# Row tiles of the token norm in the x^T buffers, double buffers for T and its copy, U and X copies of 132 columns, six PSUM places for w_in

## The chip, the cores and the metric

The kernel runs on one core of one Trainium2 chip. The metric is the device time in microseconds (us) of one execution. A time is the median of several runs of the same program. Below, PE stands for TensorE, DVE for VectorE, ACT for ScalarE, POOL for GpSimd and SP for SyncE, whose queue issues most of the DMA transfers of the first half.

## The reference

One layer of a streaming encoder is computed for 1024 prompt tokens and 32 sample tokens, 1056 columns in all. Both pass through the same layer: a norm over each token, one input projection w_in (1024 inputs), and two branches that read its output, a state-space branch (S5, 32 groups of 16 channels, 64 complex states each) and a latent attention branch (MLA). The sample tokens start from given states and a given cache.

```python
def mixer_layer(x, pos, h0, past_ckv, past_krope, p):
    h = rmsnorm(x, p['norm_in'])
    z = h @ p['w_in']
    u, g_ssm, c_q, c_kv, k_rope_raw, g_mla = jnp.split(z, cuts, axis=-1)
    y_ssm, h_last = s5_branch(u, h0, p)
    q = (rmsnorm(c_q, p['q_lora_norm']) @ p['w_uq']).reshape(...)
    ...
    mix = jnp.concatenate([rmsnorm(y_ssm, p['out_norm_ssm']) * jax.nn.silu(g_ssm),
                           rmsnorm(attn, p['out_norm_mla']) * jax.nn.silu(g_mla)], axis=-1)
    return x + mix @ p['w_out'], ckv, krope, h_last

def s5_branch(u, h0, p):
    ...
    bu = jnp.einsum('gpc,bsgc->bsgp', b_bar, ug.astype(jnp.complex64))
    _, states = lax.associative_scan(_ssm_combine, (a_seq, bu), axis=1)
    y = jnp.einsum('gcp,bsgp->bsgc', c_mat, states).real
    y = y + p['ssm_d'] * ug
    yg = jax.nn.gelu(y)
    out = yg * jax.nn.sigmoid(yg @ p['w_glu'] + p['b_glu'])
```

## The kernel before

**The input projection.** x arrives transposed, in eight tiles of 128 features by 1056 columns (`xr`). Each is split into a high and a low part (`xh` by ACT, `xl` by DVE), as are the weights (`wh`, `wl`). A tile m of w_in is 128 output rows: three PSUM chunks of 384, 384 and 288 columns, each the sum over eight k of three products (`wh*xh`, `wh*xl`, `wl*xh`), 72 matmuls named `mt` at L235 in all. The tiles m = 0 to 3 give u, eight more give the two gates. The PSUM chunks come from the tag "g" with `CAP["g"]` places. The projection runs on x without the token norm; the factor 1/rms of each token is applied when a chunk leaves PSUM (`mtile_evac`, on DVE, against the tile `rb`).

**The token norm.** x is read a second time in rows (nine tiles `xk`, 128 tokens by 1024; L279 and L282), and ACT squares and sums each at L283. DVE turns the nine sums into 1/rms (the steps from L284 to L160), and PE spreads them over the partitions (`rb_p`, L185), from where ACT copies them to `rb` (L187). Tiles m = 0 and 1 end before `rb` is there; ACT copies them raw to `ur` (L298), and DVE scales them later into `uT` (L251).

**The state-space branch.** `uT` goes to DRAM (`du`) and comes back as `U`, 16 channels by 8 steps on the partitions, 132 columns for each of the 8 groups of a tile. A block of 8 steps is one column (4 of the sample, 128 of the prompt). `ssm_in(m)` builds the weights W and transposes them to `Gt` (`gt_p`, L469), forms the kernel parts `kpt` and `kp`, and multiplies `Gt` with U to `v_p` (L491); ACT copies v_p to X (L494, L495). A scan over the blocks runs on DVE in X. Then, for each m, the output `y_p` is the sum of two matmuls for each of 8 groups, `Tg * U` (L681) and `Hm * Xc` (L682). `Tg` is a reordered copy of T by ACT (L667), `Xc` a reordered copy of the states in X by ACT (L670). T, Tg and Xc have one buffer each. ACT applies gelu into `ysb` (L683), `ysb` goes to DRAM, returns as `yg`, is split into `ygh` and `ygl`, and feeds the gated unit's matmuls `gl` (L711).

**What sets the order.** The source's order is not the order of the engines. A scheduler puts the instructions of each engine into one fixed order, by data dependencies, by how many buffers and PSUM places each tag has, and by its own model of times; each engine then runs its list in order. So a change of a buffer count moves work on every engine. Marks (`issue_after`) keep some work behind a given instruction.

Of the kernel before, what the change touches and what calls it, by code (L numbers as in the profile page):

```python
# [50 lines left out]
def step(ctx: ExitStack, tc, xT, xr, winF, winT, wuq, wukv, wglu, wout, ckvcT, krcT, pk, rot, ssb, ssc, mtab,  # L51
# [5 lines left out]
    sb = ctx.enter_context(tc.tile_pool(name="sb", bufs=1))  # L57
    sm = ctx.enter_context(tc.tile_pool(name="sm", bufs=2))
    psS = ctx.enter_context(tc.tile_pool(name="psS", bufs=2, space=PSUM))
    CAP = {"a": 6, "b": 4, "g": 4, "w": 4}  # L60
    psA = ctx.enter_context(tc.tile_pool(name="psA", bufs=4, space=PSUM))
    dr = ctx.enter_context(tc.tile_pool(name="dr", bufs=1, space=DRAM))

# [210 lines left out]

    ssx = CC(TS)
    for i in range(TS):
        t = T("xk", [128, D], 3)
        if i < 8:
            sp.dma_start(t, xr[i * 128:i * 128 + 128])  # L279
        else:  # L280
            for j in range(4):
                sp.dma_start(t[32 * j:32 * j + 32], xr[NP_:])  # L282
        act.activation(t, t, AF.Square, accum_out=ssx[:, i:i + 1])  # L283
# [163 lines left out]
    XR = X.rearrange("p g (j s) -> p g j s", j=8)  # L447

    def load_u(m, after=None):

        t = T("U", [128, 4 + 8 * NCH], 2)
        dve.memset(t[:, 0:4], 0.0)
        with tc.issue_after(marks[after]) if after else nullcontext():
            sp.dma_start(t[:, 4:].rearrange("p (g n) -> p g n", n=NCH), du[m].rearrange("r c g n -> (r c) g n"))
        return t

    def ucol(t, g):

        return t[:, g * NCH:g * NCH + 136]

    def ssm_in(m):
        w = T("W", [128, 8, 128], 2)
# [24 lines left out]
        for g0 in (0, 3, 6):  # L487
            n = min(3, 8 - g0)
            p = PA("v_p")
            for j in range(n):  # L490
                pe.matmul(p[:, j * 136:(j + 1) * 136], gt[:, g0 + j, :], ucol(u, g0 + j), start=True, stop=True)  # L491
            pb = p[:, :n * 136].rearrange("p (g s j) -> p g j s", g=n, j=8)
            xg = XR[:, 8 * m + g0:8 * m + g0 + n]
            act.activation(xg[:, :, 1:8, 0:17], pb[:, :, 0:7], AF.Copy)  # L494
            act.activation(xg[:, :, 0, 1:18], pb[:, :, 7], AF.Copy)  # L495


    aq = T("aq", [128, 3, 4, G])
# [158 lines left out]


    for m in range(4):
        Tm = T("T", [128, L, 8, GC], 1)  # L660
        for s in range(L):
            o = (L - 1 - s) * 16
            with tc.issue_after(marks["so"]):
                sp.dma_start(Tm[:, s].rearrange("p g c -> p (g c)"), dk[o:o + 128, m * 128:(m + 1) * 128])

        Tg = T("Tg", [128, 8, L, GC], 1)
        act.activation(Tg.rearrange("p g s c -> p s g c"), Tm, AF.Copy)  # L667
        hm = T("Hm", [128, 8, 128], 2)
        xc = T("Xc", [128, 8, 136], 1)
        act.activation(xc.rearrange("p g (s j) -> p g s j", j=8),  # L670
                       XR[:, 8 * m:8 * m + 8, :, 0:17].rearrange("p g j s -> p g s j"), AF.Copy)
        with tc.issue_after(marks["scan"]):
            expand(hm.rearrange("p g (s c) -> p g s c", c=GC), ct[:, 0], ct[:, 1], m, pr, pi, dve)
        u = load_u(m, "so")
        ysb = T("ysb", [128, 8, NCH], 2)
        for g0 in (0, 3, 6):
            n = min(3, 8 - g0)
            p = PA("y_p")
            for j in range(n):
                o = p[:, j * 136:(j + 1) * 136]  # L680
                pe.matmul(o, Tg[:, g0 + j].rearrange("p s c -> p (s c)"), ucol(u, g0 + j), start=True, stop=False)  # L681
                pe.matmul(o, hm[:, g0 + j, :], xc[:, g0 + j], start=False, stop=True)  # L682
            act.activation(ysb[:, g0:g0 + n], p[:, :n * 136].rearrange("p (g c) -> p g c", c=136)[:, :, 4:],  # L683
                           AF.Gelu_apprx_tanh)
        sp.dma_start(dy[m].rearrange("s c g n -> (s c) g n"), ysb)


# [650 lines left out]
```

## Time and profile before

| | |
|---|---|
| median of 3 runs | 588.09 us (587.78 to 588.16) |
| the profiled execution's own time | 588.01 us |
| its span, first to last instruction | 586.2 us |
| PE busy | 548.5 us, 94% of the span |
| DVE busy | 416.4 us, 71% |
| ACT busy | 306.7 us, 52% |
| mean granted clock of PE | 0.974 |

The span leaves 1.8 us of the profiled time outside. The granted clock has two levels, 1.0 (2.4 GHz) and 0.5 (1.2 GHz); a value between them is a stretch that holds some of each. A line's busy time is the sum of its instructions; matmuls overlap, so that the busy time of PE is the time in which any of them runs.

### The profile page before, as it was taken

How to read it: one execution, taken by the hardware profiler on the slowest of the kernel's cores; microseconds unless marked ns; L12 is line 12 of the kernel's file. 1: busy time of each engine (PE TensorE's matmuls, PEld its weight loads, DVE VectorE, ACT ScalarE, POOL GpSimd, SP SyncE). 2: the span in 40 equal slices, each digit the busy share in tenths (PEclk: the TensorE clock that was granted, in tenths of full speed). 3: DMA queues.
4: the chain of work that ended last, by engine and by line, in shares of the span. 5: the costliest groups of instructions: out<-in, count | busy, mean ns of one | idle time of the engine just before them, and what ended most of it. 6: DMA issues, size and time to landing. Idle time of an engine off the chain costs nothing.

```text
span 586.2 us, 9933 instructions
## 1 busy us (share of the span) xinstructions
PE 548.5 (94%) x3707; PEld 481.0 (82%) x3707; DVE 416.4 (71%) x1008; ACT 306.7 (52%) x647; POOL 107.1 (18%) x165
## 2 busy tenths in 40 slices
PE   5995899999999999689999799999999999999897
PEld 4995799889999998689888678887778888876785
DVE  6998533989999355038999996669798677674722
ACT  5743145127242635649855975786675776653000
POOL 0000000000000010000024520032245244458430
PEclk9998899999999999679999899999999999999999
DMA  8992642222551007352301031200100101096362
GB/s 286 397 303 45 184 148 73 79 74 88 158 176 45 0 24 215 119 181 90 122 29 72 26 107 73 92 1 2 39 20 2 38 1 40 1 341 209 105 253 107
DMA packets 35265, 63.92 MB, mean 109 GB/s; under 512 B 5361, under 2 KB 21521, under 8 KB 35217
## 3 DMA queue, kind: packets, MB, share of 16 engines
q1 hardware_dynamic: 31008, 49.06, 25.6%
q10 hardware_dynamic: 4208, 14.22, 7.0%
q8 instruction: 29, 0.48, 0.3%
q14 instruction: 20, 0.16, 0.1%
HBM read 47.06 MB, written 16.21 MB: 108 GB/s over the span
## 4 chain that ended last, share of the span: by engine, by line
PE 76%; DVE 12%; ACT 4%; DMA 3%; issue 2%; POOL 2%; SPq 1%; ACTq 0%; POOLq 0%; DVEq 0%
PE mt L235 21%; PE wo L879 9%; PE ob L1054 6%; PE pt_p L1026 5%; PE S L986 3%; PE S L987 3%; PE S L988 3%; PE gl L711 3%; PE tk_p L590 2%; PE tk_p L591 2%; PE tk_p L592 2%; PE y_p L682 1%; PE ob L1055 1%; PE v_p L491 1%; DMA wr<-winF 1%
## 5 line engine op out<-in xcount | busy, mean ns | idle before, releaser
L235 PE MATMUL mt<-xh,wh 128*128 128x384 f32 (+1 forms) x288 | 78.3, 334 | 9.0 <-ACT xh L112 6.6
L235 PE MATMUL mt<-xl,wh 128*128 128x384 f32 (+1 forms) x288 | 77.6, 330 | 0.4 <-DVE xl L113 0.4
L235 PE MATMUL mt<-xh,wl 128*128 128x384 f32 (+1 forms) x288 | 76.7, 329 | 0.0
L235 PEld LDWEIGHTS mt<-xh,wh 128*128 128x128 f32 x288 | 51.3, 191 | 11.2 <-ACT xh L112 7.2
L235 PEld LDWEIGHTS mt<-xl,wh 128*128 128x128 f32 x288 | 51.3, 192 | 1.1 <-DVE xl L113 0.7
L235 PEld LDWEIGHTS mt<-xh,wl 128*128 128x128 f32 x288 | 50.8, 192 | 0.2 <-issue 0.2
L1026 PE MATMUL pt_p<-base,P 128*128 128x128 f32 x288 | 43.1, 276 | 0.7 <-ACT kv L775 0.7
L879 PE MATMUL wo<-woh,mm 128*128 128x512 f32 x128 | 42.0, 399 | 1.2 <-DVE mm L110 1.2
L1054 PE MATMUL ob<-PT,kv 128*64 128x128 f32 x576 | 41.9, 279 | 0.9 <-DVE PT L1030 0.9
L1054 PEld LDWEIGHTS ob<-PT,kv 128*64 128x64 f32 x576 | 32.0, 136 | 10.3 <-issue 6.5
L1008 DVE TENSOR_REDUCE base<-S 128x1 f32<-128x1024 f32 (+3 forms) x32 | 32.4, 1016 | 10.5 <-PE S L988 10.4
L742 POOL TENSOR_TENSOR base<-base 128x288 f32<-128x288 f32 x1 | 0.9, 862 | 211.3 <-DVE kro L638 211.3
L1010 ACT ACTIVATE P<-S,base 128x1024 f32<-128x1024 f32 (+3 forms) x32 | 30.5, 953 | 14.9 <-DVE base L1008 14.7
L1026 PEld LDWEIGHTS pt_p<-base,P 128*128 128x128 f32 x288 | 33.0, 140 | 5.1 <-ACT kv L775 0.9
L986 PE MATMUL S<-kTh,qTh 104*128 104x512 f32 (+3 forms) x96 | 36.1, 376 | 0.0
L1030 DVE COPY PT<-pt_p 128x512 f32<-128x512 f32 (+2 forms) x44 | 27.9, 634 | 9.5 <-PE pt_p L1026 8.5
L988 PE MATMUL S<-kTh,qTh 96*128 96x512 f32 (+3 forms) x96 | 34.2, 360 | 0.0
L987 PE MATMUL S<-kTl,qTh 96*128 96x512 f32 (+3 forms) x96 | 33.4, 348 | 0.0
L109 ACT ACTIVATE wh<-wr 128x512 fp32r<-128x512 f32 x24 | 14.0, 623 | 34.2 <-PE mt L235 29.6
L879 PEld LDWEIGHTS wo<-woh,mm 128*128 128x128 f32 x128 | 24.1, 190 | 7.1 <-DVE mm L110 1.6
L109 ACT ACTIVATE wt<-wtr 128x416 fp32r<-128x416 f32 x16 | 8.6, 554 | 36.8 <-PE tk_p L592 16.1
L825 POOL TENSOR_TENSOR qx<-q,base 128x256 f32<-128x256 f32 (+1 forms) x12 | 8.6, 731 | 104.0 <-DVE base L160 88.6
(344 smaller groups left out, 1449.2 us busy)
## 6 DMA issues: line engine op xcount, KB each, us to landing
wr<-winF SPq DMA_DIRECT2D x10, 512.0 KB, 4.5
U<-du SPq DMA_DIRECT2D x8, 528.0 KB, 4.0
xk<-xr SPq DMA_DIRECT2D x8, 512.0 KB, 7.7
wor<-wout ACTq DMA_DIRECT2D x8, 512.0 KB, 4.4
dyp<-yp SPq DMA_DIRECT2D x8, 512.0 KB, 2.6
part<-dyp ACTq DMA_DIRECT2D x8, 512.0 KB, 5.5
xt<-xr ACTq DMA_DIRECT2D x8, 512.0 KB, 7.3
xr<-xT SPq DMA_DIRECT2D x7, 528.0 KB, 7.9
```

The lines of the kernel that those rows point to most:

```text
L109: act.activation(hi, src, AF.Copy)
L235: pe.matmul(ps[c][:, :b - a], ww[:, k, :], xx[k][:, a:b], start=(k == 0 and first), stop=(k == 7 and last))
L711: pe.matmul(ps[c][:, :352], ww[:, k], xx[k][:, c * 352:(c + 1) * 352], start=(k == 0 and first), stop=(k == 3 and last))
L879: pe.matmul(s[i][c], mm[i][a][k], ww[k][b][:, c * 512:(c + 1) * 512], start=(k == 0 and first), stop=(k == 3 and last))
L986: pe.matmul(s[:, :n], qh[:, qj], kh[:, j, :n], start=True, stop=False)
L987: pe.matmul(s[:, :n], qh[:96, qj], kl[:, j, :n], start=False, stop=False)
L988: pe.matmul(s[:, :n], ql[:, qj], kh[:96, j, :n], start=False, stop=True)
L1008: dve.tensor_reduce(rl[:, 2 + j:3 + j], sf, AX.X, ALU.max, negate=True)
L1010: marks["exp", u] = act.activation(t[:, :n], sf, AF.Exp, bias=rl[:, 2 + j:3 + j], accum_out=rl[:, j:j + 1]).ins
L1026: pe.transpose(pp[:, (q - b) * 128:(q - b + 1) * 128], t[:, q * 128:(q + 1) * 128], ident)
L1030: dve.tensor_copy(ov, pp[:, :(e - b) * 128])
L1054: pe.matmul(ob[64 * j:64 * j + 64, r0:r0 + 128], v, t[:, b + q], start=(q == 0), stop=(q == nb - 1))
```

## The change

Four things are changed. The places of the tag "g", for the chunks of w_in, go from 4 to 6. The row tiles of the token norm, which had three buffers of their own (`xk`), use the eight buffers of `xr`, which the tiles of x^T leave when they have been split. T and its reordered copy, which had one buffer each (`T`, `Tg`), use the two buffers of `Gt` and the two of `W`, which the weights of `ssm_in` leave. U is loaded without the four zero columns ahead of its first group, and v_p and y_p are computed on 132 columns a group in place of 136; the four columns that were computed beside them, the initial states, are now copied apart: ACT fills X with four copies for each v_p in place of two, and Xc with two in place of one.

```diff
--- before.py
+++ after.py
@@ -57,7 +57,7 @@
     sb = ctx.enter_context(tc.tile_pool(name="sb", bufs=1))
     sm = ctx.enter_context(tc.tile_pool(name="sm", bufs=2))
     psS = ctx.enter_context(tc.tile_pool(name="psS", bufs=2, space=PSUM))
-    CAP = {"a": 6, "b": 4, "g": 4, "w": 4}
+    CAP = {"a": 6, "b": 4, "g": 6, "w": 4}
     psA = ctx.enter_context(tc.tile_pool(name="psA", bufs=4, space=PSUM))
     dr = ctx.enter_context(tc.tile_pool(name="dr", bufs=1, space=DRAM))
 
@@ -274,7 +274,7 @@
 
     ssx = CC(TS)
     for i in range(TS):
-        t = T("xk", [128, D], 3)
+        t = T("xr", [128, NT], 8)[:, :D]
         if i < 8:
             sp.dma_start(t, xr[i * 128:i * 128 + 128])
         else:
@@ -447,16 +447,7 @@
     XR = X.rearrange("p g (j s) -> p g j s", j=8)
 
     def load_u(m, after=None):
-
-        t = T("U", [128, 4 + 8 * NCH], 2)
-        dve.memset(t[:, 0:4], 0.0)
-        with tc.issue_after(marks[after]) if after else nullcontext():
-            sp.dma_start(t[:, 4:].rearrange("p (g n) -> p g n", n=NCH), du[m].rearrange("r c g n -> (r c) g n"))
-        return t
-
-    def ucol(t, g):
-
-        return t[:, g * NCH:g * NCH + 136]
+        return LD("U", [128, 8, NCH], du[m].rearrange("r c g n -> (r c) g n"), 2, after)
 
     def ssm_in(m):
         w = T("W", [128, 8, 128], 2)
@@ -488,11 +479,14 @@
             n = min(3, 8 - g0)
             p = PA("v_p")
             for j in range(n):
-                pe.matmul(p[:, j * 136:(j + 1) * 136], gt[:, g0 + j, :], ucol(u, g0 + j), start=True, stop=True)
-            pb = p[:, :n * 136].rearrange("p (g s j) -> p g j s", g=n, j=8)
+                pe.matmul(p[:, j * NCH:(j + 1) * NCH], gt[:, g0 + j, :], u[:, g0 + j], start=True, stop=True)
+            pv = p[:, :n * NCH].rearrange("p (g c) -> p g c", g=n)
+            pb = pv[:, :, 4:].rearrange("p g (s j) -> p g j s", j=8)
             xg = XR[:, 8 * m + g0:8 * m + g0 + n]
-            act.activation(xg[:, :, 1:8, 0:17], pb[:, :, 0:7], AF.Copy)
-            act.activation(xg[:, :, 0, 1:18], pb[:, :, 7], AF.Copy)
+            act.activation(xg[:, :, 1:8, 1:17], pb[:, :, 0:7], AF.Copy)
+            act.activation(xg[:, :, 0, 2:18], pb[:, :, 7], AF.Copy)
+            act.activation(xg[:, :, 5:8, 0], pv[:, :, 0:3], AF.Copy)
+            act.activation(xg[:, :, 0, 1], pv[:, :, 3], AF.Copy)
 
 
     aq = T("aq", [128, 3, 4, G])
@@ -657,18 +651,19 @@
 
 
     for m in range(4):
-        Tm = T("T", [128, L, 8, GC], 1)
+        Tm = T("Gt", [128, L, 8, GC], 2)
         for s in range(L):
             o = (L - 1 - s) * 16
             with tc.issue_after(marks["so"]):
                 sp.dma_start(Tm[:, s].rearrange("p g c -> p (g c)"), dk[o:o + 128, m * 128:(m + 1) * 128])
 
-        Tg = T("Tg", [128, 8, L, GC], 1)
+        Tg = T("W", [128, 8, L, GC], 2)
         act.activation(Tg.rearrange("p g s c -> p s g c"), Tm, AF.Copy)
         hm = T("Hm", [128, 8, 128], 2)
-        xc = T("Xc", [128, 8, 136], 1)
-        act.activation(xc.rearrange("p g (s j) -> p g s j", j=8),
-                       XR[:, 8 * m:8 * m + 8, :, 0:17].rearrange("p g j s -> p g s j"), AF.Copy)
+        xc = T("Xc", [128, 8, NCH], 1)
+        xg = XR[:, 8 * m:8 * m + 8]
+        act.activation(xc[:, :, 4:].rearrange("p g (s j) -> p g s j", j=8), xg[:, :, :, 1:17].rearrange("p g j s -> p g s j"), AF.Copy)
+        act.activation(xc[:, :, 0:4], xg[:, :, 4:8, 0], AF.Copy)
         with tc.issue_after(marks["scan"]):
             expand(hm.rearrange("p g (s c) -> p g s c", c=GC), ct[:, 0], ct[:, 1], m, pr, pi, dve)
         u = load_u(m, "so")
@@ -677,11 +672,10 @@
             n = min(3, 8 - g0)
             p = PA("y_p")
             for j in range(n):
-                o = p[:, j * 136:(j + 1) * 136]
-                pe.matmul(o, Tg[:, g0 + j].rearrange("p s c -> p (s c)"), ucol(u, g0 + j), start=True, stop=False)
+                o = p[:, j * NCH:(j + 1) * NCH]
+                pe.matmul(o, Tg[:, g0 + j].rearrange("p s c -> p (s c)"), u[:, g0 + j], start=True, stop=False)
                 pe.matmul(o, hm[:, g0 + j, :], xc[:, g0 + j], start=False, stop=True)
-            act.activation(ysb[:, g0:g0 + n], p[:, :n * 136].rearrange("p (g c) -> p g c", c=136)[:, :, 4:],
-                           AF.Gelu_apprx_tanh)
+            act.activation(ysb[:, g0:g0 + n].rearrange("p a b -> p (a b)"), p[:, :n * NCH], AF.Gelu_apprx_tanh)
         sp.dma_start(dy[m].rearrange("s c g n -> (s c) g n"), ysb)
```

`LD` loads a DRAM source into a tile of the given tag, and `NCH` is 132. Lines of the changed kernel are 4 to 9 lower from `ssm_in` on: v_p is L491 before and L482 after, y_p L681 and L682 before, L676 and L677 after.

The change moves instructions. Three places matter below. The first is PE at the point where the factors of the token norm are spread (`rb_p`). The rows name the PSUM chunk and its inputs; mt_402 to 404 are m = 2, mt_491 to 493 are m = 3, mt_2011 (before) or mt_2039 (after) begin the first gate's tile. Before:

```order
L235 MATMUL mt_491<-xh_158,wh_484 128x384
L235 MATMUL mt_491<-xl_159,wh_484 128x384
L235 MATMUL mt_491<-xh_158,wl_485 128x384
L185 MATMUL rb_p_216<-base_72 128x128 x4
L185 MATMUL rb_p_222<-base_72 128x128 x4
L185 MATMUL rb_p_228<-base_72 128x32
L469 MATMUL gt_p_736<-base_72,W_730 128x128 x4
L469 MATMUL gt_p_742<-base_72,W_730 128x128 x4
L475 MATMUL kpt_748<-W_730,ct_708 32x128 x8
L480 MATMUL kp_749<-base_72,kst_758 128x128 x2
L235 MATMUL mt_492<-xh_92,wh_484 128x384
L235 MATMUL mt_492<-xl_93,wh_484 128x384
```

After:

```order
L235 MATMUL mt_493<-xl_159,wh_484 128x288
L235 MATMUL mt_491<-xh_158,wl_485 128x384
L235 MATMUL mt_492<-xh_158,wl_485 128x384
L235 MATMUL mt_493<-xh_158,wl_485 128x288
L185 MATMUL rb_p_216<-base_72 128x128 x4
L185 MATMUL rb_p_222<-base_72 128x128 x4
L185 MATMUL rb_p_228<-base_72 128x32
L460 MATMUL gt_p_736<-base_72,W_730 128x128 x4
L460 MATMUL gt_p_742<-base_72,W_730 128x128 x4
L466 MATMUL kpt_748<-W_730,ct_708 32x128 x8
L471 MATMUL kp_749<-base_72,kst_758 128x128 x2
L235 MATMUL mt_2039<-xh_92,wh_2032 128x384
```

Before, chunk mt_491 alone stands ahead of `rb_p`, and the 48 matmuls of mt_492 and mt_493 follow behind `kp`. After, all of m = 3 stands ahead, and behind `kp` come 27 matmuls of the first gate (21 of mt_2039, 3 each of mt_2040 and mt_2041), and then v_p.

The second place is ACT at the end of tiles 0 and 1 (mt_168 to 173). Before:

```order
L298 ACTIVATE ur_375<-mt_168 128x384
L298 ACTIVATE ur_375<-mt_169 128x384
L298 ACTIVATE ur_375<-mt_170 128x288
L298 ACTIVATE ur_384<-mt_171 128x384
L109 ACTIVATE wt_1067<-wtr_1065 128x416
L109 ACTIVATE wt_1088<-wtr_1086 128x416
L109 ACTIVATE wh_395<-wr_394 128x512 x2
L298 ACTIVATE ur_384<-mt_172 128x384
L298 ACTIVATE ur_384<-mt_173 128x288
L109 ACTIVATE wh_484<-wr_483 128x512 x2
```

After:

```order
L298 ACTIVATE ur_375<-mt_168 128x384
L298 ACTIVATE ur_375<-mt_169 128x384
L298 ACTIVATE ur_375<-mt_170 128x288
L283 ACTIVATE xr_180,base_72<-xr_180 128x1024
L298 ACTIVATE ur_384<-mt_171 128x384
L298 ACTIVATE ur_384<-mt_172 128x384
L298 ACTIVATE ur_384<-mt_173 128x288
L109 ACTIVATE wh_395<-wr_394 128x512 x2
L283 ACTIVATE xr_183,base_72<-xr_183 128x1024
L109 ACTIVATE wh_484<-wr_483 128x512 x2
```

Before, wh_395, the weights of m = 2, stands ahead of the copies of the last two chunks. After, it stands behind all six copies and the Square of row tile xr_180. On PE all six chunks now end within the last 18 matmuls ahead of mt_402; before, the chunks mt_172 and mt_173 stood alone in the last 48. ACT's list after goes on with the Squares of the other row tiles and then holds the weights of the second gate, wh_2121, ahead of the `rb` copies; before, these weights stood behind `kst`.

The third place is PE in the y_p stage, at the end of the first output tile. Before:

```order
L681 MATMUL y_p_1631<-U_1611,Tg_1602 128x136
L682 MATMUL y_p_1631<-Xc_1605,Hm_1604 128x136
L235 MATMUL mt_2675<-xl_118,wh_2667 128x384
L235 MATMUL mt_2676<-xl_118,wh_2667 128x288
L235 MATMUL mt_2675<-xh_117,wl_2668 128x384
L235 MATMUL mt_2676<-xh_117,wl_2668 128x288
```

After:

```order
L676 MATMUL y_p_1651<-U_1632,W_1622 128x132
L677 MATMUL y_p_1651<-Xc_1625,Hm_1624 128x132
L676 MATMUL y_p_1680<-U_1677,W_1667 128x132
L676 MATMUL y_p_1688<-U_1677,W_1667 128x132
L676 MATMUL y_p_1696<-U_1677,W_1667 128x132
L677 MATMUL y_p_1680<-Xc_1670,Hm_1669 128x132
```

Before, the last gate's tile (mt_2674 to 2676) had 45 of its 72 matmuls left here, and 26 of them stand between m = 0 and m = 1, the rest behind m = 1. After, all w_in work has ended ahead of the first y_p, and the four output tiles follow each other.

## Rows read from the trace of the kernel before

**Rows 1.** The page's first part: engine, busy us, share of the span, instructions.

```profile
PE 548.5 (94%) x3707; PEld 481.0 (82%) x3707; DVE 416.4 (71%) x1008; ACT 306.7 (52%) x647; POOL 107.1 (18%) x165
```

**Rows 2.** TensorE's waits: waiting line, releaser: us in total, times, longest.

```profile
PE mt L235 <- ACT xh L112: 6.6, 3, 4.9
...
PE y_p L681 <- ACT Tg L667: 3.3, 2, 2.1
...
PE y_p L682 <- ACT Xc L670: 2.5, 2, 1.3
```

**Rows 3.** Stretches of the span: us, busy us (instructions), clock, DMA.

```profile
33.00:48.90 15.90, 15.90 (x98) 15.69 (x96) 14.77 (x44) 9.44 (x18) 0.00 (x0) 1.00 0.82 237
48.90:55.40 6.50, 0.15 (x2) 0.06 (x2) 6.50 (x39) 0.00 (x0) 0.00 (x0) 0.91 0.00 0
55.40:61.40 6.00, 5.50 (x35) 4.06 (x35) 4.37 (x14) 2.86 (x6) 0.00 (x0) 0.53 0.22 63
...
63.80:68.00 4.20, 4.19 (x15) 4.19 (x16) 2.45 (x5) 0.00 (x0) 0.00 (x0) 0.59 0.61 156
...
73.00:217.00 144.00, 144.00 (x960) 136.83 (x959) 104.35 (x240) 57.31 (x148) 1.84 (x3) 1.00 0.28 88
...
226.30:229.70 3.40, 3.40 (x31) 3.40 (x30) 0.24 (x2) 0.50 (x1) 0.00 (x0) 1.00 0.63 150
...
235.80:242.10 6.30, 6.23 (x26) 5.91 (x26) 0.00 (x0) 3.62 (x4) 0.00 (x0) 0.51 0.11 47
...
246.30:252.50 6.20, 6.11 (x26) 5.90 (x26) 0.00 (x0) 1.71 (x4) 0.00 (x0) 0.53 0.98 279
```

**Rows 4.** TensorE in order of time: start us, length us, line, output<-inputs [idle before].

```profile
33.02 0.51 PE L235 MATMUL mt<-xh,wh 128*128 128x384 f32 x2
...
55.37 0.87 PE L185 MATMUL rb_p<-base 128*128 128x128 f32 x3 [6.35 <-DVE aq L505]
63.81 0.44 PE L235 MATMUL mt<-xh,wh 128*128 128x384 f32 x1 [2.40 <-DVE uT L251]
...
72.79 0.63 PE L491 MATMUL v_p<-U,Gt 128*128 128x136 f32 x4
...
217.62 0.40 PE L681 MATMUL y_p<-U,Tg 128*128 128x136 f32 x2
```

**Rows 5.** ScalarE in order of time, 33 to 57 us; columns as in rows 4.

```profile
33.09 0.79 ACT L298 ACTIVATE ur<-mt 128x384 f32<-128x384 f32 x2 [2.18 <-PE mt L235]
33.76 1.15 ACT L109 ACTIVATE wh<-wr 128x512 fp32r<-128x512 f32 x2
34.81 1.06 ACT L283 ACTIVATE xk<-xk 128x1024 f32<-128x1024 f32 x1
...
44.77 1.06 ACT L283 ACTIVATE xk<-xk 128x1024 f32<-128x1024 f32 x1 [3.91 <-DMA xk<-xr]
...
56.55 0.60 ACT L187 ACTIVATE rb<-rb_p 128x512 f32<-128x512 f32 x1 [8.06 <-PE rb_p L185]
```

**Rows 6.** ScalarE in order of time, first v_p and y_p stage; columns as in rows 4.

```profile
74.09 0.20 ACT L495 ACTIVATE X<-v_p 128x51 f32<-128x51 f32 x1
...
232.44 1.05 ACT L667 ACTIVATE Tg<-T 128x1024 f32<-128x1024 f32 x1
233.39 0.38 ACT L683 ACTIVATE ysb<-y_p 128x264 f32<-128x264 f32 x1
233.66 2.05 ACT L670 ACTIVATE Xc<-X 128x1088 f32<-128x1088 f32 x1
...
252.66 0.38 ACT L683 ACTIVATE ysb<-y_p 128x264 f32<-128x264 f32 x1
```

**Rows 7.** SyncE's queue in order of time: start us, length us, issue.

```profile
59.14 1.28 SPq L293 DMA_DIRECT2D du<-uT  x2
63.09 0.34 SPq L454 DMA_DIRECT2D U<-du  x1
```

**Rows 8.** DMA issues of the page: KB each, us from issue to landing.

```profile
U<-du SPq DMA_DIRECT2D x8, 528.0 KB, 4.0
```

## Prediction

> **What bounds the kernel now.** I read the page's first part first: PE is busy 94% of the span, DVE 71%, ACT 52% [rows 1]. So PE sets the time, and time can be won only where PE stands still, or where it works at the half clock. PE's own list of waits then shows where it stands still in the part that the change touches: 6.6 us at the start, for the high parts of x^T, and in the y_p stage 3.3 us for Tg and 2.5 us for Xc [rows 2]. The windows show the rest. From 48.9 to 55.4 PE works 0.15 of 6.5 us; from 55.4 to 61.4 the clock is 0.53, from 63.8 to 68 it is 0.59, and in two stretches of y_p, 235.8 to 242.1 and 246.3 to 252.5, it is 0.51 and 0.53. From 73 to 217 PE is never idle and the clock is 1.00 [rows 3]. So there are two bad places, which I call the second start (48.9 to 73) and the y_p stage (217.6 to 252.7), with a stretch of pure PE work between them.
>
> At the second start PE waits 6.35 us ahead of rb_p and then 2.40 us ahead of the next w_in matmul [rows 4]. The reader is to see that the name behind the 6.35 us, aq, is only DVE's neighbour of the 1/rms steps: those could not start before the last Square, and the Squares were late, one of them 3.91 us for its row tile [rows 5].
>
> **Prices.** At the full clock a w_in matmul costs 15.9 us / 98 = 0.162 us, a mean over the 384- and 288-column chunks [rows 3]. Between 63.8 and 68 15 of them took 4.2 us, 0.28 each. In y_p, where the trace has two records for a matmul, 31 records took 3.40 us at the full clock, 0.110 each [rows 3]. Behind the wait for Xc there are 26 of an output tile's 32 records (the first six need only Tg): 26 x 0.110 = 2.9 us at the full clock, and 6.2 us in the two slow windows, which hold just these 26 each [rows 3].
>
> **The second start.** With six PSUM places both first tiles run together, and every k that has arrived offers 18 matmuls in place of 12. Some of PE's early 6.6 us is filled: 8 matmuls, 1.3 us, is my choice (0 at least, 12 or 1.9 us at most, since two k have arrived by then). The two tiles end at 33.02 - 1.3 = 31.7.
>
> Then comes a wait that the change adds. The weights of m = 2 now stand on ACT behind six ur copies and a Square, and the first three copies can start only when their chunks end, 9 matmuls or 1.45 us before the end. ACT needs 3 x 0.40, 1.06, 3 x 0.40 and 0.58 for the first half of wh [rows 5]: 4.0 us, less 1.45, less about 0.2 of overlap: 2.4 us. Behind it on ACT are the other Squares, and on PE everything. m = 2 starts at 34.1.
>
> All of m = 2 and 3 now stands ahead of rb_p: 144 x 0.162 = 23.3, so rb_p starts at 57.4 in place of 55.37. The row tiles have all been issued by then, since none waits for one of three buffers: six Squares (1.06) and wh_484 (1.15) take 7.5 us behind 34.1 and end near 41.6, which leaves the 1/rms steps 15.8 us, so the 6.35 us are gone. But the weights of the second gate (1.15) now stand ahead of the rb copies; they start at 58.55 in place of 56.55. From the rb copies to the next w_in matmul it was 63.81 - 56.55 = 7.26 us [rows 4, 5]; the order on DVE there is the same, and with kpt at the full clock about 0.4 is saved. w_in goes on at 65.4.
>
> Up to the first v_p only 27 w_in matmuls stand in place of 48: 4.4 us, and 1.8 us more if the clock is low for as long as between 63.8 and 68 (15 x 0.162 = 2.4 against 4.2). v_p starts at V = 71.6, with 69.6 (no low clock, 0.2 less on DVE) and 73.4 (27 x 0.28, nothing saved) as its bounds; before it was 72.79 [rows 4]. U does not decide it: du went out at 59.14, U was issued 3.95 us later and took 4.0 us [rows 7, 8]; two us later that is 69.1.
>
> **Between.** From v_p to y_p PE had 144.83 us of work without a gap [rows 4]. The 45 w_in matmuls that lay in the y_p stage now lie ahead of it, and 27 have moved ahead of v_p (144 and 27, less 96 and 48): 18 more, 2.9 us. The first y_p starts at V + 147.7 = 219.3. The 24 further ACT copies into X cost 0.20 each [rows 6], 4.8 us in all; ACT was busy 57 of the 144 us [rows 3], so they are hidden, and so are the memsets that go from DVE, which was busy 104. Four columns less in 136 save 3% of 192 records of 0.11 us, 0.6 us at most if length goes with columns; I count 0, because the y_p spells are limited by the waits.
>
> **The y_p stage.** It lasted from 217.62 to 252.66, the last gelu, D = 35.04 [rows 4, 6], 7.3 of them the 45 w_in matmuls. After, only y_p is left. Xc still has one buffer: between two tiles ACT makes the last gelu 0.38, the copy of Xc 2.05 and its four columns 0.20 [rows 6], 2.63 us, and ahead of m = 1 and 2 the copy of T, 1.05. Two buffers take T and its copy off PE's path, but not off ACT's. So D = 3.5 (m = 0, 32 x 0.110) + 3.7 (1.05 + 2.63) + B + 3.7 + B + 2.63 + B + 0.2 = 13.75 + 3B, where B is the 26 records of a tile: 2.9 at the full clock, 6.2 at the half. Before, the clock was low in both tiles that followed a wait, though PE was then busy. The waits are now longer, but the first comes after 144 us of full work, and the slow spell at 63.8 ended by itself: a mean of 0.59 over 4.2 us is 3.4 us at 0.5 [rows 3]. A tile with such a spell (14 records at 0.24, then 12 at 0.110) takes 4.7. I take a mean of 5.6, D = 30.55, nearer to the two slow windows than to that spell; the bounds are 29.35 (two such tiles) and 32.35 (all at half).
>
> The Trainium skill says of such groups (TensorE: Matmul & The Clock Gate, section "HAM oscillation — how this bites in real kernels") that a wait between groups of matmuls puts the clock down, so that each next group starts slow, every time. The slow windows of y_p agree; by that rule alone D is 32.35 and the time 587.0.
>
> **The sum.** The work behind the last gelu is ordered as before, so the end moves by (V - 72.79) + 2.9 + (D - 35.04) = V + D - 104.93. With 71.6 and 30.55 that is -2.8 us on the profiled 588.01, which is 0.08 below the median: 585.2. The bounds of V and D give 582.0 to 588.8.
>
> **Rivals.** A change of 0.2%, 1.2 us, is about what a measurement of this kernel can tell from none.
>
> *The clock holds in y_p.* The stretch from 226.3 to 229.7 ran at 1.00. If the short waits don't bring the clock down, B = 2.9, D = 22.45, and the time 577.1. Against it: two tiles of three before were slow to their end.
>
> *No gain.* Every group behind a wait is slow, D = 32.35, and the second start is slow too, V = 72.5: -0.1, 587.9. What the second start wins is given back because y_p has lost its 7.3 us of filling work, and the wait of 2.4 us is a new one. The rows on the clock speak for it; against it, the spell at 63.8 that ended by itself.
>
> *Slower by the X copies.* A v_p place now comes free after four ACT copies in place of two. If the 4.8 us reach PE because the next v_p and gt_p wait for their places, -2.8 becomes +2.0: 590.0. It decides from 4.0 of the 4.8 on. Against it: ACT's idle time there.
>
> *Slower by a row tile.* The third Square now stands ahead of the weights of m = 2. If its row tile lands later than about 31.5, all of PE behind it moves by the same. A Square before waited for its tile until 44.77 [rows 5], so it is not impossible: a landing at 37 would give +2.7, 590.7, and it decides from 35.5 on. Against it: it is the third row tile in the queue as before, and the x^T buffer that it takes is left early.
>
> **How the numbers follow.** The forecast's case 0.50; the clock holds 0.10; no gain 0.20; X copies 0.12; a late row tile 0.08. Faster 0.60 (the first two), same 0.20, slower 0.20 (the last two). The range 580.5 to 590.0 leaves out most of the second case and of the last, and the worse half of the fourth; the likeliest case has 582.0 to 587.0.
>
> **What would show it.** Right: no wait of PE ahead of rb_p and a clock of 1.00 there; a wait of 2 to 3 us for ACT's wh near 32; v_p near 71.6; the first y_p near 219.3; three waits for Xc of 2.5 to 3.7 us, with half clock for 3.4 to 6.2 us behind each; the last gelu near 250. Wrong: Squares that still wait for DMA beyond 42; v_p later than 73.4; a wait of PE for X copies or weights between 73 and 217; y_p at the full clock.

## The result and the profile after

| | before | after |
|---|---|---|
| median | 587.9 us (586.09 to 589.02, 10 runs) | 584.63 us (582.25 to 586.03, 10 runs) |
| ratio, 95% interval | | 0.9947 [0.9929, 0.9964] |
| profiled execution / its span | 588.01 / 586.2 us | 584.77 / 583.0 us |
| mean granted clock of PE | 0.974 | 0.974 |

By the ratio, the change takes 3.1 us off (0.53%). The page's first part after, which answers to [rows 1]:

```profile
PE 547.1 (94%) x3707; PEld 481.5 (83%) x3707; DVE 414.8 (71%) x1000; ACT 304.4 (52%) x673; POOL 107.5 (18%) x165
```

TensorE's waits after, which answer to [rows 2] (waiting line, releaser: us in total, times, longest):

```profile
PE y_p L677 <- ACT Xc L666: 7.4, 3, 3.7
PE mt L235 <- ACT xh L112: 6.2, 3, 5.3
PE gl L705 <- ACT wg L109: 4.1, 2, 3.3
PE mt L235 <- DVE uT L251: 3.6, 1, 3.6
...
PE mt L235 <- ACT wh L109: 2.1, 1, 2.1
PE wos L863 <- DMA wor<-wout: 0.9, 2, 0.6
```

The 6.35 us ahead of `rb_p` are not in the list any more. The reader is to see what stands there in their place: 2.1 us for the weights wh, 1.2 us more than before for uT, three waits for Xc, and two waits further back in the program (gl, wos) that are longer than before. TensorE in order of time, which answers to [rows 4]:

```profile
34.37 0.76 PE L235 MATMUL mt<-xh,wh 128*128 128x384 f32 x3 [2.12 <-ACT wh L109]
...
57.68 0.49 PE L185 MATMUL rb_p<-base 128*128 128x128 f32 x3
...
66.10 0.69 PE L235 MATMUL mt<-xh,wh 128*128 128x384 f32 x1 [3.60 <-DVE uT L251]
...
73.06 0.50 PE L482 MATMUL v_p<-U,Gt 128*128 128x132 f32 x3
...
218.91 0.39 PE L676 MATMUL y_p<-U,W 128*128 128x132 f32 x2
...
227.04 0.49 PE L677 MATMUL y_p<-Xc,Hm 128*128 128x132 f32 x2 [3.70 <-ACT Xc L666]
...
234.57 0.49 PE L677 MATMUL y_p<-Xc,Hm 128*128 128x132 f32 x2 [1.99 <-ACT Xc L666]
...
241.87 0.49 PE L677 MATMUL y_p<-Xc,Hm 128*128 128x132 f32 x2 [1.76 <-ACT Xc L666]
...
248.37 0.47 PE L705 MATMUL gl<-ygh,wg 128*128 128x352 f32 x1 [3.31 <-ACT wg L109]
```

The same landmarks side by side, in us from the start of the span, with two kernels of the experiments (first start; "gl end" and "q_p end" are where the last matmul of the gated unit and of the query projection starts):

| | rb_p | v_p | y_p | last gelu | gl | gl end | q_p end | span |
|---|---|---|---|---|---|---|---|---|
| before | 55.4 | 72.8 | 217.6 | 252.7 | 254.6 | 280.9 | 319.4 | 586.2 |
| after | 57.7 | 73.1 | 218.9 | 245.1 | 248.4 | 275.2 | 316.0 | 583.0 |
| after, minus before | +2.3 | +0.3 | +1.3 | -7.6 | -6.2 | -5.7 | -3.4 | -3.2 |
| e1_places5 | 55.7 | 68.2 | 214.0 | 246.2 | 248.2 | 274.2 | 312.6 | 579.5 |
| e5_places5_rms_first | 53.3 | 67.3 | 212.2 | 245.6 | 247.5 | 273.8 | 311.9 | 579.2 |

So the second start wins nothing by itself (+0.3 at the first v_p, though 27 w_in matmuls stand ahead of it that came later before), the y_p stage is 8.9 us shorter (some 7.3 of these are w_in matmuls that now stand ahead of it), and of the 7.56 us at the last gelu 4.3 are given back before the end. The windows show why y_p is short and where some of it goes back (us, busy us (instructions) of PE, PEld, DVE, ACT, POOL, clock, DMA):

```profile
66.00:71.00 5.00, 4.90 (x15) 4.91 (x16) 3.52 (x9) 0.00 (x0) 0.00 (x0) 0.50 0.80 167
228.00:231.50 3.50, 3.50 (x19) 3.50 (x19) 0.00 (x0) 1.16 (x3) 0.00 (x0) 0.52 0.83 231
235.00:238.50 3.50, 3.50 (x19) 3.50 (x18) 1.26 (x1) 0.99 (x2) 0.00 (x0) 0.52 0.57 152
242.00:245.00 3.00, 3.00 (x26) 2.87 (x26) 1.26 (x1) 1.80 (x3) 0.00 (x0) 1.00 0.40 87
...
290.00:292.00 2.00, 2.00 (x8) 1.25 (x9) 2.00 (x4) 0.67 (x1) 0.00 (x0) 0.50 0.32 127
292.00:294.00 2.00, 2.00 (x10) 1.95 (x9) 2.00 (x6) 1.29 (x3) 0.00 (x0) 0.75 0.14 27
```

Two of the three tiles behind a wait for Xc have a stretch at half clock, of about 3.5 us and no more, and the last tile has none: its 26 records take 3.0 us. The stretch does not begin with the tile: behind the wait of 3.70 us the clock is 1.00 for the first 1.0 us, behind the one of 1.99 for the first 0.3 us.

What DVE did between the sums of squares and `rb_p` is in its order of time. L284 is the first of the twelve 1/rms steps, L160 ends each of their three rounds, and the rows between are expansions of the state-space weights (L439, L440), the powers (L364 to L369) and weight splits (L110):

```profile
45.48 0.16 DVE L284 TENSOR_SCALAR base<-base 128x9 f32<-128x9 f32 x1
45.55 1.21 DVE L440 TENSOR_TENSOR W<-W,ex 128x1024 f32<-128x1024 f32 x1
...
52.81 0.16 DVE L160 SCALAR_TENSOR_TENSOR base<-base 128x9 f32<-128x9 f32 x1
...
55.36 0.17 DVE L160 SCALAR_TENSOR_TENSOR base<-base 128x9 f32<-128x9 f32 x1
```

The first and the last of the twelve steps before:

```profile
49.85 0.16 DVE L284 TENSOR_SCALAR base<-base 128x9 f32<-128x9 f32 x1
...
55.06 0.16 DVE L160 SCALAR_TENSOR_TENSOR base<-base 128x9 f32<-128x9 f32 x1
```

And ScalarE in order of time, the last Square and the end of y_p, beside [rows 5, 6]:

```profile
43.03 1.07 ACT L283 ACTIVATE xr<-xr 128x1024 f32<-128x1024 f32 x1 [1.43 <-DMA xr<-xr]
...
245.10 0.39 ACT L678 ACTIVATE ysb<-y_p 128x264 f32<-128x264 f32 x1 [0.17 <-PE y_p L677]
246.72 1.08 ACT L109 ACTIVATE ygh<-yg 128x1056 fp32r<-128x1056 f32 x1 [1.22 <-DMA yg<-dy]
247.70 0.62 ACT L109 ACTIVATE wg<-wgr 128x512 fp32r<-128x512 f32 x1
```

The last Square before, which [rows 5] does not show (the row that waits 3.91 us there is the last but one):

```profile
47.34 1.06 ACT L283 ACTIVATE xk<-xk 128x1024 f32<-128x1024 f32 x1 [0.37 <-ACT wh L109]
```

The last Square ends at 44.1 (before at 48.4), 4.3 us earlier, and the 1/rms steps begin 4.4 us earlier (45.48; before at 49.85). But they end at 55.5, 0.3 us later than before. Twelve steps of 0.16 us are 2 us of work; they took 10, and 5.4 before.

### The profile page after: what moved, and what is told of

Read it like the earlier page. It is cut to its first block, busy times and chain, and to the rows that moved or that the text cites. A ratio compares the mean times of both kernels' runs of the same rounds, so it can differ in the third digit from the quotient of the medians.

```text
span 583.0 us, 9939 instructions
## 1 busy us (share of the span) xinstructions
PE 547.1 (94%) x3707; PEld 481.5 (83%) x3707; DVE 414.8 (71%) x1000; ACT 304.4 (52%) x673; POOL 107.5 (18%) x165
## 4 chain that ended last, share of the span: by engine, by line
PE 74%; DVE 10%; ACT 5%; DMA 5%; issue 2%; POOL 2%; SPq 1%; ACTq 0%; DVEq 0%; POOLq 0%
PE mt L235 24%; PE wo L873 11%; PE ob L1048 6%; PE pt_p L1020 5%; PE S L980 3%; PE S L981 3%; PE S L982 3%; PE tk_p L585 2%; PE tk_p L584 2%; PE tk_p L586 2%; PE gl L705 2%; DMA yg<-dy 1%; PE ob L1049 1%; PE v_p L482 1%; PE qt_p L965 1%
## 5 line engine op out<-in xcount | busy, mean ns | idle before, releaser
L235 PE MATMUL mt<-xh,wh 128*128 128x384 f32 (+1 forms) x288 | 68.5, 335 | 11.9 <-ACT xh L112 6.2
L235 PE MATMUL mt<-xl,wh 128*128 128x384 f32 (+1 forms) x288 | 68.3, 331 | 0.1
L235 PE MATMUL mt<-xh,wl 128*128 128x384 f32 (+1 forms) x288 | 67.3, 330 | 0.0
L235 PEld LDWEIGHTS mt<-xh,wh 128*128 128x128 f32 x288 | 49.8, 193 | 13.5 <-ACT xh L112 6.8
L235 PEld LDWEIGHTS mt<-xl,wh 128*128 128x128 f32 x288 | 49.8, 193 | 1.0 <-issue 0.6
L235 PEld LDWEIGHTS mt<-xh,wl 128*128 128x128 f32 x288 | 49.2, 191 | 0.2 <-issue 0.2
L1184 DVE SCALAR_TENSOR_TENSOR yp<-wo,base,xt 128x512 f32<-128x512 f32 x16 | 11.6, 749 | 21.2 <-PE wo L873 21.2
```

What stands on the lines that cost most here:

```text
L235: pe.matmul(ps[c][:, :b - a], ww[:, k, :], xx[k][:, a:b], start=(k == 0 and first), stop=(k == 7 and last))
```

## Experiments

**The second start.** The theory after the first reading of the trace: the 1/rms steps are late because DVE runs one fixed list in which they stand between expansions and powers, and PSUM places help because they put more w_in work ahead of `rb_p`. The rival is the prediction's own cause: the Squares are late because the row tiles wait for their buffers. The first two kernels part these.

e1_places5 is the kernel before with one place more, and nothing else:

```diff
-    CAP = {"a": 6, "b": 4, "g": 4, "w": 4}
+    CAP = {"a": 6, "b": 4, "g": 5, "w": 4}
```

> The kernel before with five places for w_in in place of four, and nothing else. On PE 264 w_in matmuls stand ahead of rb_p in place of 240, and 24 behind it in place of 48. Theory of the prediction (rb_p is held by the 1/rms steps, and these by Squares that wait for late row tiles): rb_p still starts near 55.4, PE's wait ahead of it shrinks from 6.35 to about 2.5 us, and since 24 matmuls less are left behind it, the first v_p moves from 72.8 to 69 to 70.5 and the time by -2 to -4 us. Rival (the order alone holds rb_p, the row tiles play no part): rb_p moves with the w_in work in front of it, and there is no wait for the 1/rms steps.

Measured: 583.22 us (581.3 to 584.59), ratio 0.9936 [0.991, 0.9962]. One number gives as much as the whole change. e2_rows_places5 adds the row tiles of the change to it:

```diff
-        t = T("xk", [128, D], 3)
+        t = T("xr", [128, NT], 8)[:, :D]
```

> As the run with five places, and the row tiles of the token norm in the eight x^T buffers. PE's list is the same up to the gated unit; only the row tiles' transfers and the Squares' places differ. Theory: no Square waits long for its row tile, the 1/rms steps end before PE needs them, the wait ahead of rb_p falls below 0.5 us, and rb_p starts at 52 to 54; a further 1.5 to 3 us are won against five places alone. Rival: the row tiles don't hold rb_p, and the two runs have the same time within 1 us.

Measured: 583.8 us, 0.9955 [0.9938, 0.9972]; the row tiles add nothing that can be measured. TensorE of e1 in order of time:

```profile
55.66 0.40 PE L185 MATMUL rb_p<-base 128*128 128x128 f32 x2 [2.34 <-DVE aq L505]
...
63.36 0.40 PE L235 MATMUL mt<-xh,wh 128*128 128x288 f32 x1 [2.41 <-DVE uT L251]
...
68.18 0.51 PE L491 MATMUL v_p<-U,Gt 128*128 128x136 f32 x3
```

The wait ahead of `rb_p` is 2.34 in place of 6.35 us, by 4 us of work put ahead of it, and with `rb_p` where it was, v_p comes 4.6 us earlier. In e2 `rb_p` starts at 54.14 behind a wait of 1.03: there the earlier row tiles give 1.5 us at `rb_p`, which are gone at the end. Further back PE of e2 waits long for mm, the split input of the output projection, where e1 waits 1.26 us:

```profile
333.94 1.22 PE L879 MATMUL wo<-woh,mm 128*128 128x512 f32 x2 [4.63 <-DVE mm L110]
```

So the two runs show that the row tiles bring nothing to the end, not that they did nothing.

To test DVE's list directly, e5_places5_rms_first takes e1 and holds the powers back until the last 1/rms step has been issued. The arithmetic is the same, and only DVE's list differs:

```diff
-    dve.tensor_copy(ar8[:, :, 0], pr[:, :, 7])
-    dve.tensor_copy(ai8[:, :, 0], pi[:, :, 7])
-    powers(ar8, ai8)
+    with tc.issue_after(marks["rst"]):
+        dve.tensor_copy(ar8[:, :, 0], pr[:, :, 7])
+        dve.tensor_copy(ai8[:, :, 0], pi[:, :, 7])
+        powers(ar8, ai8)
```

> As the run with five places alone, but DVE's work on the powers for the scan (needed only near 100 us) is held back until the 1/rms steps are issued. Only DVE's list differs; PE, ACT, POOL and SP have the same lists. In the run with five places alone rb_p started at 55.66 after a wait of 2.34 us, and in the run with the row tiles as well at 54.14 after 1.03. Theory A (DVE's list holds the 1/rms steps: they stand between other work): the steps end by 53, rb_p starts at 53.3, the wait falls below 0.5, the first v_p moves from 68.2 to 65.5 to 66.5. Theory B (the late Squares hold them, as the prediction had it): rb_p stays at 54.5 to 55.7. The time: 581 to 583.5 by A, 583 by B.

Measured: 581.01 us (580.31 to 582.32, 4 runs), 0.989 [0.9856, 0.9924]. This is below both kernels: its interval and that of the change don't meet. TensorE of e5, and the first and the last of its 1/rms steps:

```profile
53.30 0.40 PE L185 MATMUL rb_p<-base 128*128 128x128 f32 x2
...
61.42 0.61 PE L235 MATMUL mt<-xh,wh 128*128 128x288 f32 x1 [4.09 <-DVE uT L251]
...
67.35 0.39 PE L492 MATMUL v_p<-U,Gt 128*128 128x136 f32 x1
```

```profile
48.70 0.16 DVE L284 TENSOR_SCALAR base<-base 128x9 f32<-128x9 f32 x1
...
52.99 0.17 DVE L160 SCALAR_TENSOR_TENSOR base<-base 128x9 f32<-128x9 f32 x1
```

The wait ahead of `rb_p` is gone with the row tiles still in their three old buffers, where the last Square ends at 47.7: L284 starts at 48.70 and the last L160 at 52.99, 4.3 us where before took 5.2, e1 6.4 and after 9.9. Against e1, v_p is only 0.8 us earlier, since the wait for uT grew from 2.41 to 4.09: the powers now stand among the copies into uT. By medians the list is worth 2.2 us more than the place alone, but the intervals overlap, and the two profiled executions differ by 0.4 us (580.94 and 581.30). So the list is shown to hold `rb_p`; that it shortens the whole kernel is not shown. e6_rows_places5_rms_first is e5 with the row tiles of e2.

> As the last, with the row tiles in the x^T buffers too. By A and by B the 1/rms steps end before PE needs them (Squares end near 44, then some 5 us of DVE), so rb_p starts at 53 to 53.3 without a wait. By A the row tiles add nothing, the time is that of the last run within 1 us; by B it is 1 to 2.5 us shorter.

Measured: 581.91 us, 0.9912 [0.9881, 0.9943], `rb_p` at 52.86: once more nothing from the row tiles. e9_after_rms_first makes the edit of e5 in the changed kernel.

> The changed kernel, with DVE's work on the powers for the scan held back until the 1/rms steps are issued. The order on PE moves a little: rb_p behind 276 w_in matmuls in place of 288, the other 12 behind it. In the changed kernel these steps ended at 55.4 and rb_p started at 57.7, held by PE's own work. By the reading that DVE's list holds the steps: they end at 52 to 53.5, rb_p starts at 55 to 56, the first v_p moves from 73.1 to 70.5 to 72, and the time by -1 to -2.5 us against the changed kernel (584.6 to 585.0). Rival (ACT's rb copies behind the second gate's weights and the uT chain on DVE set the second start): rb_p moves, the first v_p stays within 0.5 us, the time within 1 us.

Measured: 585.57 us, 0.9953 [0.993, 0.9976], no gain over the change. TensorE of e9 in order of time:

```profile
57.39 0.38 PE L185 MATMUL rb_p<-base 128*128 128x128 f32 x2
...
60.29 0.24 PE L185 MATMUL rb_p<-base 32*128 32x32 f32 x1
...
70.20 0.69 PE L235 MATMUL mt<-xh,wh 128*128 128x384 f32 x1 [6.81 <-DVE uT L251]
```

ScalarE of e9, between the pieces of `rb`:

```profile
59.91 1.15 ACT L109 ACTIVATE wh<-wr 128x512 fp32r<-128x512 f32 x2 [0.74 <-PE mt L235]
60.97 0.18 ACT L187 ACTIVATE rb<-rb_p 128x32 f32<-128x32 f32 x1
```

The 1/rms steps end at 53, but eight of the nine matmuls of `rb_p` have 276 w_in matmuls ahead of them and stay at 57.39, and the ninth stands behind the last 12 of m = 3. ACT splits weights ahead of the last rb copy. So the end of the chain moves to 61, uT goes out later, the next copy into uT waits 1.64 us for that transfer, and PE waits 6.81 us for uT. (This execution took 588.2 us, 2.6 above the run's median.) By these rows DVE's list holds `rb_p` with five places; with six, the work that stands ahead of `rb_p` on PE and the order on ACT do.

**The 132 columns.** e11_cols132 is the kernel before with the U load, the v_p and the y_p of the change (in the diff the hunks from `load_u` on, without the new tags of T and Tg), and three places for the tag "w" in place of four.

> The kernel before with U, v_p, y_p and the copies on 132 columns, and three places in place of four for the last projection, so that it fits. The second start has the order of the kernel before, and 36 w_in matmuls still lie between the y_p tiles. Theory (the 132 columns alone bring little): 586.5 to 588.5. Rival (they carry the gain, by the shorter ACT copies of y_p): 583 to 585.5.

Measured: 592.09 us, 1.0053 [1.0024, 1.0082]; its profiled execution took 1057.45 us, so no row of it is read. e12_places5_cols132 has the same columns with five places and one raw weight buffer:

```diff
-        r = T("wr", [128, 8, 128], 2)
+        r = T("wr", [128, 8, 128], 1)
```

> Five places and 132 columns, with one buffer in place of two for the raw w_in tiles, so that it fits. Here the order differs at the second start: rb_p stands behind 226 w_in matmuls, and 38, 24 and 28 more lie behind rb_p, between the kpt matmuls and ahead of the first v_p, where the other kernels let PE wait for ACT and DVE. All w_in work ends ahead of y_p. If the 1/rms steps end at 55 as in the others, PE waits some 7 us ahead of rb_p and not at all behind it, the first v_p comes at 73 to 76, with 28 w_in matmuls more done than before: 583 to 587. If the waits behind rb_p (2.4 us) count more than the one ahead of it: 580 to 583.

Measured: 587.52 us, 0.9975 [0.9945, 1.0005]. PE waits 5.7 us for wh near the start and 8.4 us for T's copy in y_p. Each of the two gave up a buffer somewhere else, so neither prices the columns alone. That the columns are not needed for a gain of this size follows from e1, which has it without them.

**The y_p stage and behind it.** The theory: the spells at half clock follow the waits for Xc, and a shorter stage moves everything behind it. The rival: what decides when gl starts is ACT's list, in which wg stands behind the split of a tile that has yet to return from DRAM. First e3_after_again, the changed kernel once more, with no edit.

> The changed kernel once more, for a second profile. If the slow spells of the clock in the y_p stage depend on when they fall, they differ from those of the first profile (about 3.4 us in two tiles, none in the third), and the length of the stage from the first y_p to the last gelu differs from 26.2 us, by up to 6; if the spells are fixed by the program, it is 26.2 within 0.5. The same for the low clock near 290, where the first profile loses 1.5 us. The median should be 583 to 586.

Measured: 584.98 us, 0.9957 [0.9934, 0.9979]. The stage lasts 26.3 us again (219.1 to 245.4), slow after the first two waits and not after the third, so this pattern is no accident of one execution. e4_fill2 computes three T·U products a tile two times more (only in m = 1 to 3, with the same results), to keep PE busy in the waits:

```diff
+                for _ in range(2 if m and j == 0 else 0):
+                    pe.matmul(o, Tg[:, g0 + j].rearrange("p s c -> p (s c)"), u[:, g0 + j], start=True, stop=True)
```

> The changed kernel with six more matmuls (12 records, 1.3 us) in each of the three waits for Xc: the product of T and U that stands there is computed two times more into the same PSUM place and started afresh, so that the output is the same. Everything else is in the same order. The waits of PE for Xc were 3.7, 2.0 and 1.8 us, so the added work fits into them. Theory (the low clock in y_p comes from the waits): the clock falls less or later, the stage is shorter by 0 to 3 us, time -3 to 0. Rival (the spells don't depend on that, or the added work is too little): the same time within 0.5 us. If the added matmuls were on the path, +4 us.

Measured: 585.57 us, 0.9971 [0.9947, 0.9995]. Windows of e4, which answer to those of after:

```profile
229.00:231.00 2.00, 2.00 (x11) 2.00 (x11) 0.00 (x0) 0.50 (x1) 0.00 (x0) 0.50 0.78 174
...
235.00:237.00 2.00, 2.00 (x18) 2.00 (x19) 1.07 (x1) 1.40 (x2) 0.00 (x0) 1.00 0.21 31
```

The waits for Xc fell from 7.4 to 3.3 us, one of the two spells went in this execution, and the last gelu came at 243.85 in place of 245.10. It was worth nothing. TensorE of e4 at the start of gl:

```profile
248.54 0.66 PE L707 MATMUL gl<-ygh,wg 128*128 128x352 f32 x1 [4.73 <-ACT wg L109]
```

ScalarE of e4 ahead of that:

```profile
243.85 0.39 ACT L680 ACTIVATE ysb<-y_p 128x264 f32<-128x264 f32 x1 [0.17 <-PE y_p L679]
246.88 1.08 ACT L109 ACTIVATE ygh<-yg 128x1056 fp32r<-128x1056 f32 x1 [2.64 <-DMA yg<-dy]
247.87 0.61 ACT L109 ACTIVATE wg<-wgr 128x512 fp32r<-128x512 f32 x1
```

gl starts where it did, at 248.5: the wait has moved from Xc to wg, behind a ygh that waits for the third tile's return from DRAM. In this kernel the y_p stage's length no longer sets the start of gl. To move wg ahead, e8_after_wg_early loads its raw weights earlier, and needs room, which the control e7_after_sq1 has given up too:

```diff
-        sq = T("sq", [128, NT], 2)
+        sq = T("sq", [128, NT], 1)
```

> A control for the next run: the changed kernel with one buffer in place of two for the squares of the gated branch, which makes room for the next edit. The order up to the gated unit is that of the changed kernel. Expected 584 to 586, as the changed kernel.

```diff
-        split(glh, gll, LD("wgr", [128, 4, 128], wglu[m], 2, "yg2"))
+        split(glh, gll, LD("wgr", [128, 4, 128], wglu[m], 2, "yg0"))
```

> As the last, but the gated unit's weights are loaded behind the first returned output tile in place of the third. On ACT their split now stands ahead of the third output tile, and on PE 9 gl matmuls fall into the last wait for Xc. Theory (what the y_p stage wins is lost because gl waits for the weights, 3.3 us, behind the third tile's way through DRAM): no wait for wg, gl begins before 242 and goes on at 245.3, gl ends 2 to 3 us earlier, time -1.5 to -3 against the control. Rival (gl then waits for the fourth tile, which sets its end anyway): the time of the control within 0.7 us.

Measured: e7 588.53 us, 1.0013 [0.9984, 1.0042]; e8 585.06 us, 0.9943 [0.9917, 0.9968]. The buffer alone cost 3.5 us, which was not expected, and the early weights gave as much back. The trace of e7 shows a place where it can be lost: at the end of q_p it is level with the change (315.8 and 316.0), and then it waits for mm, where the change waits 0.26 us:

```profile
339.99 1.22 PE L873 MATMUL wo<-woh,mm 128*128 128x512 f32 x2 [4.90 <-DVE mm L110]
```

TensorE of e8:

```profile
240.96 0.41 PE L705 MATMUL gl<-ygh,wg 128*128 128x352 f32 x1
...
256.82 0.66 PE L705 MATMUL gl<-ygh,wg 128*128 128x352 f32 x1 [3.29 <-ACT ygh L109]
```

gl now starts inside the last wait for Xc and then waits 3.29 us for the fourth tile. Its last matmul starts at 274.9 (277.5 in e7), of which 1.1 us were won ahead of `rb_p` (59.9 and 58.8). So some 1.5 us were won behind it: the wait for wg was real, but most of it moved to the next return from DRAM. e10_places5_rms_first_wg_early is e5 with the same early load, and three places for "w".

> Five places, 1/rms steps first (581.0), and the gated unit's weights loaded behind the first returned output tile; the places for the last projection go from four to three, so that it fits. Theory: gl no longer waits for its weights (2.0 us), 9 of its matmuls fill the last wait of the y_p stage, 1.5 to 3 us are won: 578 to 580. Rival (the fourth tile's way through DRAM sets the end of gl, and the fewer places cost something at the end): 580.5 to 583.

Measured: 584.12 us, 0.9931 [0.9899, 0.9962]. At q_p's end it is 3.0 us ahead of e5 (308.9), at the end of the span 3.5 us behind it (582.7); a wait of 3.3 us for mm and one of 1.9 us for ssa are new or longer. Which part of that the place taken from "w" cost wasn't tried apart. Nor were the double buffers of T and its copy alone, the row tiles alone at four places, or a second buffer for Xc.

## Why the prediction came out, point by point

**The total** was 585.2 and is 584.63, but two terms behind it were off by over 4 us each, with opposite signs. In its own sum, against the profiled execution: V 73.06 for 71.6 (+1.5); between, 145.85 for 147.7 (-1.9); D 26.19 for 30.55 (-4.4); and behind the last gelu, counted as unchanged, +4.3. That is -0.4, from 585.2 to 584.77. So the total is near by luck: the two large errors nearly cancel.

**The cause at the second start was wrong.** "The Squares were late" held the 6.35 us in the prediction's reading. The rows of after refute it (the Squares end and the 1/rms steps begin over 4 us earlier, but the steps end 0.3 later), and e5 shows what holds `rb_p`: the order of DVE's list. Of the 6.35 us the Squares had some 1 to 1.5: DVE of before sat idle for 1.03 us until the last but one of them ended, and e2, where they come earlier, has `rb_p` 1.5 us earlier than e1. One of the prediction's own signs of being wrong, a Square that waits for DMA beyond 42, came up (the last waited 1.43 us, until 43.03) and decided nothing.

What the prediction built on the cause came right all the same, since `rb_p` has so much PE work ahead of it that it would not have noticed: the wait for wh 2.12 (2.4 predicted) at 34.37 (34.1), `rb_p` at 57.68 (57.4), the rb copies at 58.45 (58.55). The filling of PE's early waits was worth 0.4 us and not 1.3 (6.2 for 6.6). V was 1.5 us off by two other terms. "The order on DVE there is the same" was not so: a weight split now stands ahead of uT, and the next copy into uT waits until an earlier uT has gone to DRAM:

```profile
65.48 1.35 DVE L251 TENSOR_TENSOR uT<-mt,rb 128x384 f32<-128x384 f32 x3 [0.71 <-DMA du<-uT]
```

So PE waits 3.60 and w_in goes on at 66.10 (65.4). Then 5 us at half clock (the window from 66 to 71) made the 27 matmuls 6.96 us long (6.2), and put v_p at 73.06, near the bound without a gain, 73.4.

**Between.** The first y_p came at 218.91 (219.3). The 18 matmuls moved into this stretch were counted at the mean of all chunks; 14 of them have 288 columns. That explains some of the 1.9 us; the rest stays open. The ACT copies and memsets were hidden, as predicted: there is no wait for X in the list.

**The y_p stage** had the right mechanism and a size outside its bounds, D 26.19 against 29.35 to 32.35. In the terms of the prediction's sum, the part without B came right: the first 32 records 3.60 us (3.5), the last gelu 0.2 (0.2), and from the end of a tile to the first Xc product of the next 4.53, 2.83 and 2.60 (3.7, 3.7 and 2.63), 13.76 in all for 13.75. PE's listed waits are shorter (3.70, 1.99 and 1.76), because the next tile's first six T·U records, 0.84 us, run inside each of these stretches. The first stretch is longer because ACT comes to it late (its first gelu starts at 222.92, behind a table load), the second shorter because T's copy lay beside PE's slow work. What failed is B, the 26 records of a tile: 4.70, 4.70 and 3.03 us for a mean of 5.6. The two slow tiles were as long as the prediction's shorter spell (4.7), which it used for its lower bound alone, and the tile at full clock lay outside the bounds. Why a spell ends within a tile here, when both slow tiles before were slow to their end, is open.

The Trainium skill's page "TensorE: Matmul & The Clock Gate", section "HAM oscillation — how this bites in real kernels", tells of a kernel in which every group of matmuls starts cold, each behind a wait that is long enough; the prediction takes it without that condition. The trace agrees only in part: two tiles ran slow (0.52 for 3.5 us), though not from their start and one of them behind 1.99 us only, and the tile behind 1.76 us did not (1.00).

**"The work behind the last gelu is ordered as before, so the end moves by" the same was a step that failed.** The order is the same, but the waits are not. The difference in the table shrinks from -7.6 to -6.2 at gl, whose weights stand on ACT behind ygh; that waits for a return from DRAM. In e4 the stage ended 1.25 us earlier and gl didn't; in e8 gl began early and waited for the next return. Some 2.3 us more go between gl's end and q_p's end: PE waits 0.9 us for wor (0.3 before), and the clock, 1.00 in all of 286 to 294 before, falls to 0.50 at 290. That the waits for wor bring the clock down is argued from their place, not tested.

**The rivals.** That the clock holds in y_p came true for one tile of three. X copies and a late row tile did not show: PE has no idle time from 73 to 219, and the third Square, ahead of the weights of m = 2, waits for nothing (31.57). "No gain" was right in its parts at the second start, and wrong in y_p.

**What carries the gain.** Five places alone give 0.9936 [0.991, 0.9962], the whole change 0.9947 [0.9929, 0.9964], but not in the same place: e1 has its first v_p 4.6 us earlier than before and a y_p stage of 32.2 us, the change gains nothing at v_p and has a y_p stage of 26.2 us. Row tiles (e2, e6) add nothing at the end that was measured. The columns (e11, e12) were not priced apart, nor were the double buffers. So that a place is enough for such a gain is shown; which edits carry the changed kernel's own gain is not. The lowest median is that of e5, 581.01 us.

## What to carry to other kernels

When an engine waits for a chain of tiny steps, read the list of the engine that runs them before blaming their inputs: twelve steps of 0.16 us took 5.4 us before and 10 after, because long work stood between them, and 4.5 in e5, where some of that work was held back and the wait for them went. A forecast that moves everything behind a stage by the same amount needs a look at the first wait behind it; if it is for a transfer, the shorter stage meets a longer wait. And when one edit among four is a buffer count, run it alone first.

## What the runs showed of the hardware that was not expected

The clock fell without a long wait. After waits of 0.34 and 0.58 us TensorE of after did 16 products for a row sum, one column each:

```profile
287.54 0.64 PE L863 MATMUL wos<-wor,base 128*32 128x256 f32 x8 [0.58 <-DMA wor<-wout]
288.11 2.27 PE L170 MATMUL rsy_p<-base,ssy 128*128 128x1 f32 x16
```

It was busy all of 288 to 294, and the clock went from 1.00 to 0.50 (0.89, 0.50 and 0.75 in three windows of 2 us). Before, the same 16 products stood at 293.08 behind no wait, and the clock stayed at 1.00, so the products alone do not bring it down; that the short waits do is argued. In e3, the same program, the low stretch there was longer (0.90, 0.50, 0.50, 0.50, 0.89 from 288 to 298), and q_p ended 1.8 us later. Such spells may be part of why executions of one kernel differ by some 4 us.
